# Wider output columns, interleaved memory heads and a reordered first projection in a fused two-stack transformer kernel

## The chip, the cores and the metric

The kernel runs on one core of a Trainium2 chip. The metric is the device time of one execution in microseconds; the value of a kernel is the median of several runs.

## What is computed

Two networks follow each other; the second takes the first one's output as its `x`. All weights and activations are fp32, 512 tokens of width 1024.

```python
# first block: one layer
h = rmsnorm(x, g_mix)
rq, rk, rv, rg, nq, nk, nv, xq, gate_logits = split(h @ w_in)
y_ret = (silu(rg) * groupnorm(retention(rq, rk, rv, forward and backward))) @ w_ret_o
y_na  = neighbourhood_attention(nq, nk, nv, na_rpb) @ w_na_o           # 8 heads of 64
y_xa  = cross_attention(xq, rmsnorm(mem, g_mem) @ w_mem_kv) @ w_xa_o   # 4 heads of 128, 256 memory rows
g_ret, g_na, g_xa = split(sigmoid(gate_logits))
x = x + (g_ret * y_ret + g_na * y_na + g_xa * y_xa) @ w_out
x = rmsnorm(x + moe(rmsnorm(x, g_ffn)), g_final)                       # 16 experts, 2 per token
# second block: two layers; ctx has 256 rows, x 512
for l in range(2):
    mod = silu(c) @ w_ada[l] + b_ada[l]          # shifts, scales, gates; the same for c_ctx
    h, hc = modulated rmsnorm of x and of ctx
    q, k, v of h and hc through w_in[l] (three attention kinds), joint attention over x and ctx
    x  = x + gate * rms(attention @ w_out[l])    # ctx too in layer 0
    x  = x + gate * rms(swiglu ffn)              # ctx too in layer 0
```

## The kernel before, in words

Every fp32 product is made of three: `split` (L87, lines 91 and 92) and `pair` (L73, lines 81 and 82) divide an operand into a high part, written by ACT, and a low part, written by DVE, and `mm3` (L97, lines 99 to 101) multiplies high by high, one high by low and low by high into one PSUM tile. A weight group is a 128x2048 block of 1 MB: SP's queue loads it into one of three `raw` buffers (L68), ACT makes `whi`, DVE makes `wlo` (three of each). `ahead` (L61) asks for a weight before its user is written. The loads of `ada` use the same `raw` buffers.

`tr` is a transpose on TensorE (PE, profile line 131). `mm` (L111) hands out PSUM tiles of 512 columns, one bank each. The code is written in an order, but a scheduler decides the order of each engine from the dependencies and the buffers; each engine then runs its own list in order. `skew` (L1412) writes the stages of a loop shifted against each other.

`bg` (L1329) runs one step of `ada` (L1260), a generator that computes the modulation vectors of the second block: a step loads 1 MB of `w_ada` and issues four products. `bg` is called at many places of the first block, so that these steps fill pauses.

The stages, with the time of the profiled execution:

- Retention to 235 us; its gate uses `proj_b` (L304), which makes 128 tokens by 256 columns with 24 products, then an eviction. Four groups of 256 columns, four token tiles each. `branch_out` (L491) to 320: for each group of 256 of the 1024 output columns, `proj_a` (L318) makes the gate, 128 columns by 512 tokens at a time, and the eviction adds the branch's own product (`bo`).
- Neighbourhood attention (`neighbourhood`, L538): `nv` by `proj_b` (370 to 395), then 16 `pairs` (L613: scores two steps ahead, softmax in `exps`, transposes `prt`, products with the values). Then `memory_rows` (L650) normalizes the memory rows on ACT and DVE, `rows_to_T` transposes the output, and `branch_out` for NA runs, with `memory_keys` (L666) in its middle (456 to 557). `memory_attention` (L693) projects `xq`, runs 8 `pairs` (582 to 612.5: `xs` scores, `prt`, `xpo`) and its own `branch_out`.
- `b1_out` (L731): `w_out` in four groups of 256 columns (687 to 738), with `context_T` between; routing; 16 experts (`experts`, L1111: gate and up products `eg`, transposes `et`, down products `ed`), 795 to 1101. Ahead of the last expert `gathered` runs, which asks for the gathered rows and calls `context_T` (L1453: transposes of 256 context rows and their modulation in `modulated`, L1355, lines 1369 to 1375). The combine adds expert rows (line 1077) and uses the context for first products of the second block.
- The second block: `project` (L1503), attention, `attn_out` (L1995), `ffn`, twice. In layer 1, six tiles of 128 rows (four of `x`, two of `ctx`) meet three groups of 256 columns first (7, 5 and 6), while the last turn of layer 0's `ffn` still delivers the normalized rows (`turn` at line 1352, transposes, `modulated`). That is 2156.7 to 2222. There `rows` is called for group 7 with tiles 0 to 3 and once more, with no weight given, for tiles 4 and 5, so its weight is loaded and split twice. Each of these weights is split in four steps of 512 columns:

```python
for g, ev in first:
    rows(g, range(4), ev)
    if g == 7:
        rows(g, range(4, 6), ev)
```

`attn_out` multiplies six (layer 0) or four (layer 1) tiles by `w_out2`, in four groups of 256 columns; `take` multiplies by a gate on DVE (line 2015) and `sumsq` squares on ACT (line 164).

Of the kernel before, what the change touches and what calls it, by code (L numbers as in the profile page):

```python
# [8 lines left out]
F = mybir.dt.float32  # L9
# [28 lines left out]
class Kern:  # L38
# [298 lines left out]
    def retention(self):  # L337
# [128 lines left out]
        for j in range(4):  # L466
            def evac(t, p, j=j):
                yy = y[:, t, j * 256:j * 256 + 256]
                th = self.t5("th", F, (256,))
                nc.scalar.activation(th, p, AF.Tanh, scale=0.5)  # L470
                sg = self.t5("sg", F, (256,))
# [19 lines left out]
    def branch_out(self, yT, nk, wname, gate_group, first=False, middle=lambda: None):  # L491
# [4 lines left out]
        for g in range(4):  # L496
            if g == 2:
                middle()
            if g * 256 % nw == 0:
                w = self.W(self.i[wname][g * 256 // nw, 0], k=nk)  # L500

            def evac(f, p, g=g, w=w):
                mx = self.mixT[:, 2 * g + f]
# [13 lines left out]
            self.proj_a(gate_group + g, evac)  # L517
# [20 lines left out]
    def neighbourhood(self):  # L538
# [13 lines left out]
        for c in range(2):  # L552
            self.proj_b(16 + c, lambda t, p, c=c: nc.scalar.activation(v[:, t, c * 256:c * 256 + 256], p, AF.Copy))
# [39 lines left out]
        self.pairs(16, scores, values, ("w_na_o", (0, 0), 4), ("w_in", (24, 0), 8), ("w_in", (25, 0), 8))  # L593
# [4 lines left out]
        oT = self.rows_to_T(o[:, ::-1])  # L598
        self.branch_out(oT, 4, "w_na_o", 24, middle=lambda: self.memory_keys(rows))
# [13 lines left out]
    def pairs(self, n, scores, values, *chunks):  # L613
# [5 lines left out]
        for i in range(n + 1):  # L619
# [17 lines left out]
            if i % 2 or n == 8:  # L637
                self.bg()
# [54 lines left out]
    def memory_attention(self):  # L693
# [29 lines left out]
        self.pairs(8, scores, values, ("w_xa_o", (0, 0), 4), ("w_in", (28, 0), 8), ("w_in", (29, 0), 8))  # L723
# [7 lines left out]
    def b1_out(self, *stages):  # L731
# [6 lines left out]
        self.xss = self.small.tile([128, 4, 4], F, name="xss", bufs=1)  # L738
# [4 lines left out]
        weight = lambda c: self.W(self.i["w_out"][c, 0], k=8)  # L743

        def product(t, c, w):
            p = self.mm("wo")[:, :256]
            for kt in range(8):
                ts = slice(t * 128, t * 128 + 128)
# [6 lines left out]
        for c in range(2):  # L755
            w = weight(c)
            for t in range(4):
                product(t, c, w)
# [1490 lines left out]
```

## Time and profile before

| what | us |
|---|---|
| median of three runs (lowest, highest) | 2984.36 (2974.34, 2985.76) |
| the profiled execution, its time and its span | 2978.37, 2976.6 |
| PE busy | 2847.3 |
| DVE busy | 1766.0 |
| ACT busy | 1293.1 |
| granted clock of PE, mean | 0.98 |

"Busy" of PE includes time in which a product is on its way; products overlap, so the step from one start to the next is the cost of one. The granted clock is the share of 2.4 GHz; 0.5 is 1.2 GHz. "[2.91 <-ACT hT L1374]" behind an instruction says that its engine stood idle for 2.91 us and that ACT's write of `hT` at line 1374 ended it. `x8` joins eight equal instructions.

### The profile page before, as it was taken

The page shows a single profiled execution, that of the slowest core. Times are in us where ns is not written, and L with a number is a line of the kernel's source. Part 1 is how long each engine was busy: PE and PEld are TensorE (multiplying, and loading weights), DVE is VectorE, ACT ScalarE, POOL GpSimd, SP SyncE. Part 2 cuts the span into 40 slices and gives each one's busy share as a digit, 9 for nine tenths or more (in the row PEclk, how much of TensorE's full clock was granted, in tenths as well). Part 3 has the DMA queues.
Part 4 walks back from the last instruction along what each step waited for, and adds up shares of the span by engine and source line. Part 5 has one row for each costly group of instructions (what it writes and reads, how often), then busy time and mean ns, then how long its engine had stood idle before and what let it go on. Part 6 is the DMA issues. An engine that isn't in the chain of part 4 may idle for free. (4 is left out here: it accounts for less than half of the span.)

```text
span 2976.6 us, 44654 instructions
## 1 busy us (share of the span) xinstructions
PE 2847.3 (96%) x17896; PEld 2463.2 (83%) x17896; DVE 1766.0 (59%) x3244; ACT 1293.1 (43%) x2272; POOL 214.7 (7%) x282
## 2 busy tenths in 40 slices
PE   8999999999799998899999999999989999899998
PEld 6997777779798978888889888888878878888887
DVE  6663244346588877688857343434566798644445
ACT  3222243234477765388845121112342787432222
POOL 2200000000110022111000000000010110000000
PEclk8999999999899999999999999999989999899999
DMA  5433454364799972431014111212233300322221
GB/s 202 142 131 132 153 198 185 144 234 151 260 390 385 380 269 96 155 84 28 4 57 156 57 71 57 71 57 71 79 126 117 109 23 2 128 106 107 86 98 71
DMA packets 130083, 399.77 MB, mean 134 GB/s; under 512 B 62199, under 2 KB 74887, under 8 KB 93128
## 3 DMA queue, kind: packets, MB, share of 16 engines
q1 hardware_dynamic: 116206, 350.04, 32.9%
q0 software_dynamic: 13520, 46.55, 4.7%
q8 instruction: 143, 2.34, 0.3%
q14 instruction: 70, 0.57, 0.1%
q10 hardware_dynamic: 144, 0.26, 0.0%
HBM read 356.64 MB, written 39.39 MB: 133 GB/s over the span
## 5 line engine op out<-in xcount | busy, mean ns | idle before, releaser
L82 DVE TENSOR_TENSOR wlo<-raw,whi 128x2048 fp32r<-128x2048 f32 (+1 forms) x200 | 420.5, 2104 | 292.1 <-ACT whi L81 291.7
L81 ACT ACTIVATE whi<-raw 128x2048 fp32r<-128x2048 f32 (+1 forms) x200 | 351.0, 1762 | 495.0 <-PE fd L101 132.2
L101 PE MATMUL fg<-hT,wlo 128*128 128x512 f32 (+1 forms) x1120 | 388.0, 347 | 0.0
L100 PE MATMUL fg<-hT,whi 128*128 128x512 f32 (+1 forms) x1120 | 387.8, 346 | 0.0
L99 PE MATMUL fg<-hT,whi 128*128 128x512 f32 (+1 forms) x1120 | 387.7, 347 | 0.0
L100 PEld LDWEIGHTS fg<-hT,whi 128*128 128x128 f32 x1120 | 212.3, 190 | 29.3
L99 PEld LDWEIGHTS fg<-hT,whi 128*128 128x128 f32 x1120 | 210.9, 189 | 29.4
L101 PEld LDWEIGHTS fg<-hT,wlo 128*128 128x128 f32 x1120 | 210.7, 188 | 29.0
L2099 DVE TENSOR_TENSOR sg<-sg,fg 128x512 f32<-128x512 f32 (+1 forms) x70 | 40.1, 573 | 284.6 <-PE fg L101 284.6
L92 DVE TENSOR_TENSOR pelo<-tp,pehi 128x512 fp32r<-128x512 f32 x260 | 175.0, 683 | 13.9 <-ACT pehi L91 11.8
L101 PE MATMUL fd<-whi,hl 128*128 128x512 f32 x440 | 174.0, 395 | 0.0
L100 PE MATMUL fd<-wlo,hh 128*128 128x512 f32 x440 | 173.5, 394 | 0.0
L99 PE MATMUL fd<-whi,hh 128*128 128x512 f32 x440 | 173.4, 394 | 0.0
L91 ACT ACTIVATE pehi<-tp 128x512 fp32r<-128x512 f32 x260 | 153.8, 601 | 44.9 <-PE tp L131 43.6
L2066 DVE TENSOR_TENSOR acc<-acc,fd 128x512 f32<-128x512 f32 x180 | 120.7, 685 | 68.2 <-PE fd L101 68.2
L1903 DVE TENSOR_REDUCE smx<-sn 128x1 f32<-128x768 f32 x160 | 151.7, 949 | 12.7 <-PE sn L1897 11.7
L131 PE MATMUL tp<-ident,pn 128*128 128x128 f32 x960 | 149.0, 274 | 1.6 <-DVE pelo L92 1.2
L1906 ACT ACTIVATE pn<-sn,smx 128x768 f32<-128x768 f32 x160 | 143.9, 904 | 9.2 <-DVE smx L1903 5.6
L99 PE MATMUL eg<-whi,xt 128*96 128x256 f32 x512 | 147.0, 287 | 0.0
L100 PE MATMUL eg<-wlo,xt 128*96 128x256 f32 x512 | 145.1, 283 | 1.0 <-DVE wlo L82 1.0
L101 PE MATMUL eg<-whi,xt 128*96 128x256 f32 x512 | 144.9, 283 | 0.0
L82 DVE TENSOR_TENSOR wlo<-rawx,whi 128x2048 fp32r<-128x2048 f32 x58 | 132.9, 2292 | 20.1 <-ACT whi L81 20.1
(655 smaller groups left out, 7305.6 us busy)
## 6 DMA issues: line engine op xcount, KB each, us to landing
raw<-in_w_in SPq DMA_DIRECT2D x53, 1024.0 KB, 4.9
raw<-in_w_ada SPq DMA_DIRECT2D x48, 1024.0 KB, 5.2
raw<-in_f_gate SPq DMA_DIRECT2D x22, 1024.0 KB, 4.8
raw<-in_f_up SPq DMA_DIRECT2D x22, 1024.0 KB, 4.8
raw<-in_f_down SPq DMA_DIRECT2D x22, 1024.0 KB, 4.8
rawx<-in_e_gate SPq DMA_DIRECT2D x19, 1024.0 KB, 9.0
rawx<-in_e_up SPq DMA_DIRECT2D x19, 1024.0 KB, 9.4
rawx<-in_e_down SPq DMA_DIRECT2D x18, 1024.0 KB, 8.9
```

Source lines behind the costliest of these rows:

```text
L81: keep(nc.scalar.activation(hi[:, c], raw[:, c], AF.Copy))
L82: keep((eng or nc.vector).tensor_tensor(lo[:, c], raw[:, c], hi[:, c].bitcast(F), op=OP.subtract))
L91: nc.scalar.activation(hi, src, AF.Copy)
L92: nc.vector.tensor_tensor(lo, src, hi.bitcast(F), op=OP.subtract)
L99: t.matmul(ps, lh, rh, start=first, stop=False)
L100: t.matmul(ps, lh, rl, start=False, stop=False)
L101: t.matmul(ps, ll, rh, start=False, stop=last)
L131: self.nc.tensor.transpose(out, in_, self.ident[:k, :k])
L1903: nc.vector.tensor_reduce(m[:, t:t + 1], p[:, :768], axis=AX.X, op=OP.max, negate=True)
L1906: nc.scalar.activation(P[t], p[:, :768], AF.Exp, bias=m[:, t:t + 1], accum_out=su[:, t:t + 1])
L2066: nc.vector.tensor_tensor(acc[:, t, cs], acc[:, t, cs], p, op=OP.add)
L2099: nc.vector.tensor_tensor(sg, sg, pp[1], op=OP.mult)
```

## The change

Line numbers grow by 8 early and by 54 to 62 later (L81 becomes L89, L91 becomes L99, L1128 becomes L1182, L1375 becomes L1430).

1. `W2` loads half of the k range of two weight groups into one `raw`, so that a product has 512 columns; the retention gate and `nv` (`proj_2`), `w_out` and `w_out2` in both layers use it.
2. `branch_out` becomes a generator, `branch_steps`. `memory_keys` stands directly behind the NA pairs, and NA's steps run between the `xa` pairs, two to a pair. `w_mem_kv` is asked for ahead in place of `w_na_o` and `w_in`. These steps call no `bg`.
3. `context_T` is called behind the last expert's transposes.
4. Layer 1's first projections put two tiles of 256 columns into one bank, load each of the three weights once, and do the context tiles of group 7 last.

```diff
+    def W2(self, aps, half):
+        raw = self.wp.tile([128, 2048], F, name="raw", tag="raw", bufs=self.NRAW)
+        c = slice(half * 1024, half * 1024 + 1024)
+        for a in range(2):
+            self.nc.sync.dma_start(raw[:, a * 1024:a * 1024 + 1024], aps[a][:, c])
+        return [x.rearrange("p (a k n) -> p k a n", a=2, k=4) for x in self.pair(raw)]
...
+    def proj_2(self, g, evac):
+        ps = []
+        for half in range(2):
+            w = self.W2([self.i["w_in"][g + a, 0] for a in range(2)], half)
+            for t in range(4):
+                if half == 0:
+                    ps.append(self.mm("prj"))
+                for k in range(4):
+                    kt = 4 * half + k
+                    self.mm3(ps[t].rearrange("p (a n) -> p a n", a=2), self.h(0, kt, t * 128, t * 128 + 128),
+                             self.h(1, kt, t * 128, t * 128 + 128), w[0][:, k], w[1][:, k], kt == 0, kt == 7)
+                if half == 1:
+                    evac(t, ps[t])
+            self.bg()
...
-            self.proj_b(8 + j, evac)
+            self.proj_2(8 + 2 * j, evac)
...
+    def branch_out(self, *args, **more):
+        for i, _ in enumerate(self.branch_steps(*args, **more)):
+            if i % 4 == 3:
+                self.bg()
+    def branch_steps(self, yT, nk, wname, gate_group, first=False):
...
+            wg = self.w_in(gate_group + g)
+            for f in range(2):
+                p = self.mm("prj")
...
+                yield
+                if f == 1 and g < 3:
+                    self.ahead(("w_in", (gate_group + g + 1, 0), 8))
+                mx = self.mixT[:, 2 * g + f]
                 py = self.mm("bo")
...
+                yield
...
-        self.pairs(16, scores, values, ("w_na_o", (0, 0), 4), ("w_in", (24, 0), 8), ("w_in", (25, 0), 8))
+        self.pairs(16, scores, values, beside, ("w_mem_kv", (0, 0), 8), ("w_mem_kv", (1, 0), 8), ("w_mem_kv", (2, 0), 8))
...
-        oT = self.rows_to_T(o[:, ::-1])
-        self.branch_out(oT, 4, "w_na_o", 24, middle=lambda: self.memory_keys(rows))
+        self.na_out = self.branch_steps(self.rows_to_T(o[:, ::-1]), 4, "w_na_o", 24)
+        self.memory_keys(rows)
...
-        self.pairs(8, scores, values, ("w_xa_o", (0, 0), 4), ("w_in", (28, 0), 8), ("w_in", (29, 0), 8))
+        def beside(i):
+            next(self.na_out, None)
+            self.bg()
+            next(self.na_out, None)
+        self.pairs(8, scores, values, beside)
+        for _ in self.na_out:
+            pass
+        self.ahead(("w_xa_o", (0, 0), 4), ("w_in", (28, 0), 8))
...
+        def turned_context():
             self.hc = self.context_T()
-        self.experts(idx, y_d, ahead, y15, spreading, gathered)
+        self.experts(idx, y_d, ahead, y15, spreading, gathered, turned_context)
...
         turn(prev[1], 1, prev[2])
+        behind_last()
...
+            def pairs(g, t0, ev, w):
+                p = self.mm("prj")
+                for a in range(2):
+                    ts = slice((t0 + a) * 128, (t0 + a) * 128 + 128)
+                    for kt in range(8):
+                        self.mm3(p[:, a * 256:a * 256 + 256], hT[0][:, kt, ts], hT[1][:, kt, ts], w[0][:, kt], w[1][:, kt],
+                                 kt == 0, kt == 7)
+                for a in range(2):
+                    ev(t0 + a, p[:, a * 256:a * 256 + 256])
+            ws = []
             for g, ev in first:
-                rows(g, range(4), ev)
-                if g == 7:
-                    rows(g, range(4, 6), ev)
+                ws.append(self.W(self.i["w_in2"][l, g], k=8, steps=4))
+                for t0 in (0, 2):
+                    pairs(g, t0, ev, ws[-1])
+            pairs(7, 4, ev_g, ws[0])
...
-        weight = lambda c: self.W(self.i["w_out2"][l, c], k=8)
+        weight = lambda c, half: self.W2([self.i["w_out2"][l, 2 * c + a] for a in range(2)], half)
```

`w_out` and the rest of `attn_out` change in the same way as `proj_2`: the four tiles (in layer 0 six) of the first 512 columns are open at once while the two halves of k pass, and the second 512 columns go tile by tile with both halves at hand; `take` adds or multiplies 512 columns at a time.

How the order of the instructions moves. First ACT in the `xa` pairs (`xpr` is the exponential, `prT` the copy of a transposed tile, `whi` a weight's high part, `gate` the tanh of a branch's gate). Before:

```order
L81 ACTIVATE whi<-raw 128x2048
L608 ACTIVATE xpr,ssu<-xs,snm 128x256 x2
L630 ACTIVATE prT<-prt 128x512
L1305 ACTIVATE adar<-ada 128x512
L608 ACTIVATE xpr,ssu<-xs,snm 128x256 x2
L630 ACTIVATE prT<-prt 128x512
L608 ACTIVATE xpr,ssu<-xs,snm 128x256 x2
L630 ACTIVATE prT<-prt 128x512
L81 ACTIVATE whi<-raw 128x2048
L608 ACTIVATE xpr,ssu<-xs,snm 128x256 x2
L630 ACTIVATE prT<-prt 128x512 x3
```

With the change:

```order
L645 ACTIVATE xpr,ssu<-xs,snm 128x256 x6
L667 ACTIVATE prT<-prt 128x512
L89 ACTIVATE whi<-raw 128x2048
L535 ACTIVATE gate<-prj 128x512
L645 ACTIVATE xpr,ssu<-xs,snm 128x256 x2
L667 ACTIVATE prT<-prt 128x512
L535 ACTIVATE gate<-prj 128x512
L645 ACTIVATE xpr,ssu<-xs,snm 128x256 x2
L667 ACTIVATE prT<-prt 128x512
L89 ACTIVATE whi<-raw 128x2048
L535 ACTIVATE gate<-prj 128x512
L645 ACTIVATE xpr,ssu<-xs,snm 128x256 x2
```

NA's gates and the splits of its weights now stand between the softmax steps, where there were two splits of weights for later stages and an eviction of `ada`.

DVE at the last expert (`eg` is the product of gate and up, `hidT` the low part of its transpose, `pre` and `hc` the context's modulation and its low part). Before:

```order
L1371 TENSOR_SCALAR pre<-trp,pre_a_3881,mod_566 128x128
L1128 TENSOR_TENSOR eg<-eg 96x256
L82 TENSOR_TENSOR wlo<-raw,whi 128x2048 x2
L1375 TENSOR_TENSOR hc<-pre,hc 128x4x128 x4
L1128 TENSOR_TENSOR eg<-eg 96x256
L92 TENSOR_TENSOR hidT<-et,hidT 128x192
L82 TENSOR_TENSOR wlo<-raw,whi 128x2048
L92 TENSOR_TENSOR hidT<-et,hidT 128x192
```

With the change:

```order
L90 TENSOR_TENSOR wlo<-raw,whi 128x2048 x3
L1182 TENSOR_TENSOR eg<-eg 96x256
L90 TENSOR_TENSOR wlo<-raw,whi 128x2048 x2
L1182 TENSOR_TENSOR eg<-eg 96x256
L100 TENSOR_TENSOR hidT<-et,hidT 128x192
L90 TENSOR_TENSOR wlo<-raw,whi 128x2048
L100 TENSOR_TENSOR hidT<-et,hidT 128x192
L1426 TENSOR_SCALAR pre<-trp,pre_a_3543,mod_566 128x128 x3
L90 TENSOR_TENSOR wlo<-raw,whi 128x2048
```

The four `hc` splits no longer stand ahead of the last `eg` product; the context's work follows the last `hidT`.

ACT in layer 1's first projections (`whi` in quarters is a weight of these projections, `pre` and `hT` belong to a row tile's turn, `sqj` to its norm). Before:

```order
L1374 ACTIVATE hT_15605<-pre 128x4x128 x2
L164 ACTIVATE sqj,pss_20822<-acc 128x1024
L1369 ACTIVATE pre<-trp,mod_3887,pre_a_5718 128x128 x4
L1374 ACTIVATE hT_15605<-pre 128x4x128 x2
L81 ACTIVATE whi<-raw 128x512 x4
L164 ACTIVATE sqj,pss_20878<-acc 128x1024
L81 ACTIVATE whi<-raw 128x512 x4
L1369 ACTIVATE pre<-trp,mod_3887,pre_a_5718 128x128 x4
L1374 ACTIVATE hT_15605<-pre 128x4x128 x2
```

With the change:

```order
L1429 ACTIVATE hT_15047<-pre 128x4x128 x2
L172 ACTIVATE sqj,pss_19932<-acc 128x1024
L1424 ACTIVATE pre<-trp,mod_3549,pre_a_11970 128x128 x4
L1429 ACTIVATE hT_15047<-pre 128x4x128 x2
L89 ACTIVATE whi<-raw 128x512 x4
L172 ACTIVATE sqj,pss_19988<-acc 128x1024
L1424 ACTIVATE pre<-trp,mod_3549,pre_a_11970 128x128 x3
L1588 ACTIVATE prj<-prj 128x128 x2
L1588 ACTIVATE prj<-prj 128x256
L1429 ACTIVATE hT_15047<-pre 128x4x128
```

One of the two sets of four splits ahead of the last tile's `pre` is gone.

## Rows read from the trace of the kernel before

**Rows 1.** Page, sections 1 and 2: busy time; granted clock by slice:
```profile
PE 2847.3 (96%) x17896; PEld 2463.2 (83%) x17896; DVE 1766.0 (59%) x3244; ACT 1293.1 (43%) x2272; POOL 214.7 (7%) x282
...
PEclk8999999999899999999999999999989999899999
```

**Rows 2.** Stretches: us, PE PEld DVE ACT POOL busy, clock, DMA share:
```profile
582.00:612.50 30.50, 27.93 (x200) 19.08 (x197) 16.65 (x37) 16.94 (x44) 2.57 (x5) 0.94 0.69 254
606.00:610.50 4.50, 3.72 (x19) 2.06 (x20) 0.82 (x3) 0.12 (x1) 0.00 (x0) 0.62 0.62 213
1101.00:1150.00 49.00, 41.15 (x276) 35.79 (x275) 40.29 (x110) 29.28 (x72) 1.85 (x3) 0.93 0.39 142
2156.70:2198.20 41.50, 27.43 (x168) 25.44 (x167) 34.21 (x104) 24.80 (x63) 5.49 (x11) 0.79 0.53 187
2198.20:2222.00 23.80, 23.80 (x204) 23.80 (x203) 7.85 (x11) 8.87 (x20) 0.00 (x0) 1.00 0.24 78
```

**Rows 3.** Timeline of PE (start, length, what): two products of `w_out`:
```profile
687.46 0.28 PE L99 MATMUL wo<-whi,mTh 128*128 128x256 f32 x1
...
693.33 0.28 PE L100 MATMUL wo<-wlo,mTh 128*128 128x256 f32 x1
```

**Rows 4.** Timeline of PE: two 512-column products of `proj_a`:
```profile
575.23 0.39 PE L101 MATMUL prj<-hTh,wlo 128*128 128x512 f32 x1
...
580.67 0.39 PE L101 MATMUL prj<-hTh,wlo 128*128 128x512 f32 x1
```

**Rows 5.** Tile `wo` and line 92 by form: min/median/max ns:
```profile
L2015 DVE TENSOR_TENSOR yB<-wo,gt x40: 412/424/425, 1539.5 to 2587.6; 128x256 f32<-128x256 f32 x40
...
L92 DVE TENSOR_TENSOR pelo<-tp,pehi x260: 644/681/694, 1268.1 to 2525.4; 128x512 fp32r<-128x512 f32 x130
```

**Rows 6.** Timeline of PE, `xa` pairs: [idle before <- what ended it]:
```profile
606.78 1.94 PE L1301 MATMUL ada<-raw,silu_c 128*32 128x512 f32 x8 [2.30 <-DMA raw<-in_w_ada]
```

**Rows 7.** Timelines of DVE and PE behind the NA pairs:
```profile
459.63 1.42 DVE L663 TENSOR_SCALAR xr<-xr,mem_y 128x1024 f32<-128x1024 f32 x2
...
454.58 1.92 PE L131 MATMUL trp<-ident,mix 128*128 128x128 f32 x16
```

**Rows 8.** Page, section 6: loads, issue to landing; lines 81, 82 by form:
```profile
raw<-in_w_in SPq DMA_DIRECT2D x53, 1024.0 KB, 4.9
raw<-in_w_ada SPq DMA_DIRECT2D x48, 1024.0 KB, 5.2
...
L81 ACT ACTIVATE whi<-raw x200: 612/1916/1966, 20.4 to 2939.2; 128x2048 fp32r<-128x2048 f32 x88, 128x512 fp32r<-128x512 f32 x12
...
L82 DVE TENSOR_TENSOR wlo<-raw,whi x200: 676/2292/2761, 30.6 to 2941.1; 128x2048 fp32r<-128x2048 f32 x88, 128x512 fp32r<-128x512 f32 x12
```

**Rows 9.** Timeline of PE where layer 0's attention starts:
```profile
1254.96 0.50 PE L1897 MATMUL sn<-mhi 96*128 96x512 f32 x1 [1.52 <-DVE mlo L92]
...
1258.61 0.83 PE L131 MATMUL tp<-ident,mqrow 128*96 128x128 f32 x6 [1.27 <-DMA mkrow<-p_d]
```

**Rows 10.** Timelines of DVE and PE at the last expert:
```profile
1089.72 2.52 DVE L1375 TENSOR_TENSOR hc<-pre,hc 128x512 fp32r<-128x512 f32 x4
1092.17 0.41 DVE L1128 TENSOR_TENSOR eg<-eg 96x256 f32<-96x256 f32 x1
...
1092.63 0.58 PE L131 MATMUL et<-ident,eg 96*128 96x96 f32 x2 [5.46 <-DVE eg L1128]
```

**Rows 11.** Layer 1's first projections: timeline of PE; DVE's costliest group:
```profile
2166.32 0.48 PE L99 MATMUL prj<-whi,hT 128*128 128x256 f32 x1 [2.91 <-ACT hT L1374]
...
2175.39 0.38 PE L99 MATMUL prj<-whi,hT 128*128 128x256 f32 x1 [3.28 <-ACT hT L1374]
...
2184.18 1.97 PE L131 MATMUL trp<-ident,raw 128*128 128x128 f32 x8 [3.18 <-DVE raw L1352]
...
2196.32 0.39 PE L99 MATMUL prj<-whi,hT 128*128 128x256 f32 x1 [1.12 <-ACT hT L1374]
...
L82 DVE TENSOR_TENSOR wlo<-raw,whi 128x512 fp32r<-128x512 f32 x12 | 8.2, 686 | 0.5 <-ACT whi L81 0.5
```

More of the change, by code (lines that the diff above doesn't have):

```diff
@@ L551, in neighbourhood @@
         v = self.s8("nv", [4, 512], F)
-        for c in range(2):
-            self.proj_b(16 + c, lambda t, p, c=c: nc.scalar.activation(v[:, t, c * 256:c * 256 + 256], p, AF.Copy))
+        self.proj_2(16, lambda t, p: nc.scalar.activation(v[:, t], p, AF.Copy))
         vs = self.s8("nvs", [3, 512], F)
@@ L611, in exps, with pairs @@
         return rec
-    def pairs(self, n, scores, values, *chunks):
+    def pairs(self, n, scores, values, beside, *chunks):
         nc = self.nc
@@ L636, in pairs @@
                 chunks = chunks[1:]
-            if i % 2 or n == 8:
-                self.bg()
+            beside(i)
     def rows_to_T(self, o):
@@ L721, in values, with beside @@
                                     rec[:, :, None].to_broadcast([128, 2, 128]), op=OP.mult)
[L723 removed]
+        def beside(i):
+            next(self.na_out, None)
+            self.bg()
+            next(self.na_out, None)
[3 more added lines that the diff above has]
+        self.ahead(("w_xa_o", (0, 0), 4), ("w_in", (28, 0), 8))
         if self.stop == "xa":
@@ L742, in b1_out, with weight, product, take @@
         self.context_rows()
[L743 to L748, printed above, removed]
-                self.mm3(p, mT[0][kt // 4][:, kt % 4, ts], mT[1][kt // 4][:, kt % 4, ts], w[0][:, kt], w[1][:, kt],
+        def weight(c, half):
+            return self.W2([self.i["w_out"][2 * c + a, 0] for a in range(2)], half)
+        def product(p, t, half, w):
+            ts = slice(t * 128, t * 128 + 128)
+            for k in range(4):
+                kt = 4 * half + k
+                self.mm3(p.rearrange("p (a n) -> p a n", a=2), mT[0][half][:, k, ts], mT[1][half][:, k, ts], w[0][:, k], w[1][:, k],
                          kt == 0, kt == 7)
-            cs = slice(c * 256, c * 256 + 256)
+        def take(p, t, c):
+            cs = slice(c * 512, c * 512 + 512)
             nc.vector.tensor_tensor(xr[t][:, cs], p, xr[t][:, cs], op=OP.add)
-            self.sumsq(xr[t][:, cs], 256, self.xss[:, t, c:c + 1])
-        for c in range(2):
-            w = weight(c)
+            self.sumsq(xr[t][:, cs], 512, self.xss[:, t, c:c + 1])
+        ps = [self.mm("wo") for _ in range(4)]
+        for half in range(2):
+            w = weight(0, half)
             for t in range(4):
-                product(t, c, w)
+                product(ps[t], t, half, w)
+                if half == 1:
+                    take(ps[t], t, 0)
         self.hc = self.context_T()
-        ws = [weight(c) for c in (2, 3)]
+        ws = [weight(1, half) for half in range(2)]
         def products(t):
-            for c in (2, 3):
-                product(t, c, ws[c - 2])
+            p = self.mm("wo")
+            for half in range(2):
+                product(p, t, half, ws[half])
+            take(p, t, 1)
         self.ahead(("w_in2", (0, 0), 8))
@@ L1109, in next_weight, with experts @@
         return w
-    def experts(self, idx, y_d, ahead, y15, middle, before_last):
+    def experts(self, idx, y_d, ahead, y15, middle, before_last, behind_last):
         nc, n = self.nc, self.CAP
@@ L2037, in products @@
         def products(t):
-            for c in (2, 3):
-                p = self.mm("wo")[:, :256]
-                for kt in range(8):
-                    mms(p, ws[c - 2], t, kt)
-                take(p, t, c)
+            p = self.mm("wo")
+            for kt in range(8):
+                mms(p, ws[kt // 4], t, kt)
+            take(p, t, 1)
         self.skew(nq, products, lambda t: turns.append(self.post(l, "a", t, o[:, t], ss[:, t], xs[t], hT)),
```

49 lines of the change are left out of this document (21 added, 28 removed).

## The prediction

> **What bounds the kernel now.** I read the page first: TensorE (PE) is busy 96% of the span, DVE 59%, ACT 43% [rows 1]. So time can come from three sources only: from PE's own instructions, from the few places where PE stands still, or from stretches at a low clock; a slice that shows 7 or 8 in place of 9 has lost clock [rows 1]. Next I read the timeline of PE stage by stage, and then the table of stretches for those that the change touches [rows 2]. There the picture is not that of the mean. In layer 1's first projections (2156.7 to 2198.2) PE is busy 27.4 of 41.5 us at a mean clock of 0.79, and DVE 34.2: DVE sets that stretch. In the `xa` pairs (582.0 to 612.5) no engine is full and PE ends them late. In the combine (1101 to 1150) DVE is busy 40.3 of 49 us, nearly as long as PE. In the first projections behind the last turn (2198.2 to 2222.0) PE never stops [rows 2].
>
> The profiled execution took 2978.37 us; the three timed runs have a median of 2984.36. The four together have a mean of 2980.7, and from that the sum is taken. 0.5% is 14.9 us, about what a measurement of this kernel can tell from no change; beyond that I call it faster or slower.
>
> **Part A, 512 columns.** It removes 1920 products of 256 columns (384 in the retention gate, 192 in `nv`, 384 in `w_out`, 576 and 384 in layers 0 and 1 of `attn_out`) and adds 960 of 512. The products overlap, so their cost is the step from start to start, not the printed length. 49 steps lie between the two rows of `w_out`: 5.87 us, 0.1198 each [rows 3]. 24 steps lie between the two rows of `proj_a`: 5.44 us, 0.2267 each [rows 4]. Two narrow ones less one wide one give 0.0129 us; the first block has 480 such pairs: 6.2 us. In layer 1 the narrow step is shorter, 23.8 us for 204 [rows 2], 0.1167, which leaves 0.0067 a pair and 3.2 us for the 480 pairs of `attn_out`. Against it, what follows a last product is longer: a take of 256 columns lasts 0.42 us on DVE, an operation on 512 columns 0.68 [rows 5]. Only the ends of `w_out` and the two `attn_out` have nothing behind them, 0.3 to 0.5 us each with ACT's half of it: 1.3. The weights arrive as two half loads in place of one, with equal bytes and an equal number of splits, so nothing else changes. A = -6.2 - 3.2 + 1.3 = **-8** (-9 to -5).
>
> These rows are at odds with a rule. The Trainium skill ("TensorE: Matmul & The Clock Gate", section "Back-to-back issue gap") puts the step at the columns over 2.4 GHz plus about 2.5 ns; by it a pair would give only 2.5 ns, all 960 together 2.4 us. The trace disagrees: its narrow step is some 10 ns above that page's. The sum goes by the rows; the other outcome is a rival.
>
> **Part B, memory heads and NA's output.** In the order of the change, gates of the NA branch stand between the softmax steps of the `xa` pairs. What those pairs can give back: 30.5 us now hold 2.57 idle [rows 2], of which 2.30 at one place, waiting for a `w_ada` load [rows 6], and a stretch of 4.5 us at 0.62 that loses 1.7 [rows 2]: at least 4.3. At most: 48 products of `xs`, 32 transposes and 64 `xpo` at 0.12 are 17.3, and 56 `ada` products at half the 1.94 us for 8 of [rows 6] (they ran at 1.2 GHz) are 6.8: 24.1 of 30.5, so 6.4. I take -6, since 24 to 28 us of NA's own products now fill the pauses.
>
> New is an exposed chain. Behind the NA pairs the memory keys come at once, and their transposes need rows that line 663 scales until 461.05, two times 0.74 behind the NA evictions of DVE, while the transposes of `o` end at 456.50 [rows 7]. Today NA's gate products cover this. Two `ada` groups of about 0.97 each remain as cover, so PE stands some 2.6 us; a pause of 2.3 was followed by 1.7 us of lost clock above. Between +1 (the scaling goes earlier without the NA splits in front) and +5: +3.5.
>
> The NA steps do not call `bg`, so four calls are missing and two `ada` steps come late, in the first products of layer 0's attention. On SP's queue the `w_ada` load of the second stands between the `p_d` stores; its buffer is that of the first. A load lands 5.2 us after its issue [rows 8]; PE waits for 2 to 3 of these, and runs 1 us of products and 1.3 of copy and transposes. It absorbs the 1.52 and 1.27 that PE waits there now [rows 9]. Behind PE stand `sn` and everything after. 2.5 + 2.3 - 2.8 = +2 (0 to +4). B = -6 + 3.5 + 2 = **-0.5** (-6 to +5).
>
> **Part C, context behind the last expert.** Now DVE's four `hc` splits (1089.72 to 1092.17) stand ahead of the product that PE's `et` transposes wait for: PE is idle 5.46 us [rows 10]. In the new order that product follows directly on a `wlo` split, so `et` comes up to 2.5 us earlier, and 16 context transposes cover 1.9 of the next wait. But the same DVE work, 8 x 0.4 of `pre` and 4 x 0.65 of `hc`, goes into the combine, where DVE has 8.7 us left of 49 [rows 2], behind two additions of rows (1.3 each) and a split of 2.29 [rows 8]. If all of it lands on the path it costs 5.8, if none, the gain is 4. Take **0** (-4 to +5).
>
> **Part D, layer 1's first projections.** The three groups are 336 products: 39.2 us at 0.1167; with 32 transposes at 0.12 [rows 7] that is 43.0 of 65.3 us [rows 2]. 22.3 us are lost: PE waits for `hT` or for the scaled rows again and again, 2.91, 3.28, 3.18 and 1.12 us [rows 11], and the clock falls. DVE paces it. The change removes the second load of group 7, with it four splits on DVE, 2.7 us of the 8.2 there [rows 11], and four of 0.61 on ACT [rows 8]. In the order they stand right before the last turn's scaling, so its transposes come that much earlier. And it puts more products ahead of that turn: 193 stand before the last transposes where 110 stood, filling pauses that were there anyway; 143 are left behind them. DVE's 34.2 less 2.7, plus the 2 to 5 us that it must still wait for ACT and PE, puts the last `hT` at 2190 to 2193; 143 x 0.1167 = 16.7 more gives 2207 to 2210 in place of 2222. If DVE's wait is covered entirely, PE alone needs 43 us: 2200. So -12 to -15, -22 at the best; at the worst the 2.7 of the splits and the last pause, -4. Take **-15**, since products that fill pauses also keep the clock up. Two tiles in one bank make the eviction of the first wait for the second's 24 products, 2.8 us, but nothing on PE waits for these evictions; the stops above are all for `hT`.
>
> A rule speaks against it: the Trainium skill ("Perfetto Trace Analysis", section "Matmuls") wants independent groups in different banks, so that the eviction of one runs beside the next group. If PE had to wait 2.8 us for each of the seven pairs, 19.6 us would eat the gain; no row here shows PE waiting for a bank in this stretch.
>
> **Sum.** -8 - 0.5 + 0 - 15 = -23.5; 2980.7 - 23.5 = 2957.
>
> **The rivals.**
> 1. DVE paces the first projections as before, and a wait takes the place of the one removed: D gives its worst value, -4, A its -8, B and C together +2. -10: **2971**, no change by the bound. For it: DVE's 31.5 us of work remains in front of the last `hT`. Against: the pauses that PE has there are filled by its own products.
> 2. Slower. Between the `xa` pairs, NA's six weights (four `w_in`, two `w_na_o`) are loaded just ahead of use: 4.9 to land, 1.92 to split on ACT and 2.29 on DVE [rows 8] are 9.1 us, and a step has less than 6 us of PE work ahead of it. If SP issues each only when its user is next, 6 x 9.1 = 54.6 us are exposed in place of the 6 gained: 2980.7 - 8 + 5.5 - 15 + 54.6 gives **3018**. It decides where the issue stands under 9.1 us ahead of the first product. Against it: three raw buffers let the issue run ahead of the splits, and DMA's share in the pairs is 0.69 with room left [rows 2].
> 3. The wide step gives only 2.4 us in all, as by the rule in part A: -17.9, **2963**. Against it are the two rows' steps; the chance stands for a narrow step that the trace shows too long in stages where PE waits for something else.
> 4. D and B come out at their best, -22 and -6: -8 - 6 - 22 = -36, **2945**.
>
> **How the numbers follow.** Forecast 0.56, rival 1 0.20, rival 2 0.05, rival 3 0.12, rival 4 0.07. Rivals 3 and 4 and the forecast lie beyond 14.9 us: faster 0.75; rival 1 is the same: 0.20; slower 0.05. The forecast's own range comes from the bounds of B, C and D, about 12 to either side: 2945 to 2969. The range given takes in rivals 1, 3 and 4 and the spread of the runs (2974 to 2986) about the base: 2938 to 2975; rival 2 and some edges of the others are outside.
>
> **What would show it.** A: the wide step at 0.227, and `w_out` shorter by 2.5 us. B: PE without a stop in the `xa` pairs, a pause of 2 to 3 us behind NA's transposes, and two `ada` groups after 1240 us. C: the stop before the last `et` at about 3 us, and the combine no longer than its 49 us. D: two sets of four narrow splits in place of three, and the first projections in 47 to 53 us in place of 65. The prediction is wrong if the first projections still take over 60 us, or if PE shows stops of over 5 us before NA's products between the pairs.

## The result, and the profile after

The changed kernel takes 2966.18 us (median of 19 runs, 2957.86 to 2975.78); before, measured beside it, 2980.93 (19 runs). The ratio is 0.9949, 95% interval 0.9937 to 0.9961: 14.8 us less (11.6 to 18.8), against 23.5 forecast and inside the stated range. A second measurement of the same program, in the last series below, gave 0.9979 (0.9964 to 0.9994), 6 us less. The two intervals do not meet, so two series of the same program can differ by more than an interval says. The change is a gain, and it is smaller than the forecast.

The profiled execution has a span of 2964.5 us, 12.1 less than before. The page, sections 1 and 2:

```profile
PE 2839.2 (96%) x16936; PEld 2412.8 (81%) x16936; DVE 1760.1 (59%) x3196; ACT 1284.1 (43%) x2200; POOL 219.3 (7%) x282
...
PEclk8999999999899999999999999999999999899999
```

The 960 instructions fewer on PE are those of part A, and the slices with a low clock are one fewer [rows 1]. That says little of where the time went. I put stages side by side by the starts and ends of their products in the two timelines of PE:

| stage, by PE's products | before | after | change | forecast |
|---|---|---|---|---|
| A: retention gate, first product to the transposes of its output | 56.0 | 53.6 | -2.4 | -2.5 |
| A: `nv`, with the NA projections | 76.2 | 75.0 | -1.2 | -1.25 |
| B: last `npo` to last `xpo` (memory, `xq`, `xa` pairs; NA's output also lies here) | 158.0 | 152.3 | -5.6 | -2.5 |
| A: `w_out`, first to last product | 49.7 | 53.4 | +3.8 | -2.5 and a tail |
| C: first `gt` to last `ed` (experts) | 306.1 | 299.5 | -6.7 | 0 for C in all |
| C and B: last `ed` to the first score of layer 0 | 153.9 | 168.7 | +14.9 | +2 for B |
| A: `attn_out`, layer 0, to the first `fg` | 79.5 | 77.3 | -2.2 | -1.9 and a tail |
| D: the 336 first products of layer 1 | 65.3 | 46.4 | -18.9 | -15 |
| A: `attn_out`, layer 1, to the first `fg` | 61.6 | 63.5 | +1.9 | -1.3 and a tail |

Six lines went about as forecast or better, and three did not: `w_out`, the start of layer 0's attention, and the end of layer 1's `attn_out`. The stretches of the changed kernel that answer to [rows 2]; columns as there:

```profile
510.50:605.10 94.60, 93.80 (x516) 71.74 (x516) 35.44 (x63) 26.83 (x55) 2.57 (x5) 1.00 0.44 165
680.50:734.00 53.50, 49.21 (x223) 41.03 (x220) 33.07 (x76) 19.93 (x37) 4.75 (x9) 0.94 0.46 177
2158.60:2205.00 46.40, 43.81 (x372) 42.35 (x371) 39.21 (x109) 30.18 (x75) 5.88 (x11) 1.00 0.49 173
```

In the `xa` pairs with NA's products between them PE now stands for 0.8 of 94.6 us, at full clock. The first projections (2158.6 to 2205.0) have PE busy 43.8 of 46.4 us at full clock, where it was 27.4 of 41.5 at 0.79 in the first part alone. `w_out` (680.5 to 734.0) lost 4.3 us to standing and some of its clock; before, the stop at the same place was 0.31 us:

```profile
711.27 1.97 PE L131 MATMUL trp<-ident,x 128*128 128x128 f32 x16 [0.31 <-DVE x L1451]
```

The timeline of PE in the changed kernel, at the places where terms of the sum stand:

```profile
459.43 1.72 PE L139 MATMUL trp<-ident,xr 128*128 128x128 f32 x14 [1.49 <-DVE xr L699]
...
702.16 0.39 PE L109 MATMUL wo<-whi,mTl 128*128 128x512 f32 x1
706.83 3.68 PE L139 MATMUL trp<-ident,x 128*128 128x128 f32 x16 [4.29 <-DVE x L1506]
...
1083.33 0.38 PE L139 MATMUL et<-ident,eg 96*128 96x96 f32 x2 [1.13 <-DVE eg L1182]
...
1256.54 1.06 PE L1356 MATMUL ada<-raw,silu_c 128*32 128x512 f32 x8 [2.52 <-DMA raw<-in_w_ada]
1258.38 1.11 PE L139 MATMUL ada<-ident,adar 128*128 128x128 f32 x4 [0.77 <-ACT adar L1360]
1259.77 0.80 PE L1965 MATMUL sn<-mhi 96*128 96x512 f32 x1 [0.28 <-DVE mod L1365]
...
2166.49 0.39 PE L107 MATMUL prj<-whi,hT 128*128 128x256 f32 x1 [1.33 <-ACT hT L1429]
...
2183.30 1.09 PE L139 MATMUL trp<-ident,raw 128*128 128x128 f32 x8 [0.96 <-DVE b_y L159]
...
2577.44 1.94 PE L139 MATMUL trp<-ident,raw 128*128 128x128 f32 x8 [6.05 <-DVE post_t L163]
```

The stop for the memory rows is 1.49 us (2.6 were reckoned). The stop ahead of the last `et` went from 5.46 [rows 10] to 1.13. The four long stops of layer 1's first projections [rows 11] are one of 1.33 and one of 0.96. New are 4.29 us ahead of the context transposes in `w_out`, and 2.52 and 0.77 around an `ada` step ahead of the first score. The stop behind layer 1's `attn_out`, 4.55 us before, is 6.05.

The wide step of `w_out` is what [rows 4] said; 24 steps between these two rows of PE are 5.45 us, 0.2271 each:

```profile
681.75 0.40 PE L109 MATMUL wo<-whi,mTl 128*128 128x512 f32 x1
...
687.20 0.39 PE L109 MATMUL wo<-whi,mTl 128*128 128x512 f32 x1
```

In the `attn_out` of layer 1 it is longer, 14 steps in 3.26 us, 0.2329 each:

```profile
2567.73 0.40 PE L107 MATMUL wo<-whi,hT 128*128 128x512 f32 x1
...
2570.99 0.40 PE L109 MATMUL wo<-whi,hT 128*128 128x512 f32 x1
```

### The profile page after: what moved, and what is told of

Its sections match the earlier page's. It is cut to its first block, busy times and chain, and to the rows that moved or that the text cites. A ratio compares the mean times of both kernels' runs of the same rounds, so it can differ in the third digit from the quotient of the medians.

```text
span 2964.5 us, 42595 instructions
## 1 busy us (share of the span) xinstructions
PE 2839.2 (96%) x16936; PEld 2412.8 (81%) x16936; DVE 1760.1 (59%) x3196; ACT 1284.1 (43%) x2200; POOL 219.3 (7%) x282
## 5 line engine op out<-in xcount | busy, mean ns | idle before, releaser
L89 ACT ACTIVATE whi<-raw 128x2048 fp32r<-128x2048 f32 (+1 forms) x196 | 349.2, 1785 | 504.1 <-PE fd L109 132.3
L99 ACT ACTIVATE pehi<-tp 128x512 fp32r<-128x512 f32 x260 | 153.8, 601 | 48.4 <-PE tp L139 47.0
L1971 DVE TENSOR_REDUCE smx<-sn 128x1 f32<-128x768 f32 x160 | 151.8, 949 | 14.4 <-PE sn L1965 13.5
## 6 DMA issues: line engine op xcount, KB each, us to landing
rawx<-in_e_up SPq DMA_DIRECT2D x19, 1024.0 KB, 10.4
```

Of the source, the lines that this page charges most:

```text
L89: keep(nc.scalar.activation(hi[:, c], raw[:, c], AF.Copy))
L99: nc.scalar.activation(hi, src, AF.Copy)
L1971: nc.vector.tensor_reduce(m[:, t:t + 1], p[:, :768], axis=AX.X, op=OP.max, negate=True)
```

## The experiments

The first four take one part of the change each and put it alone on the kernel before. The edits are the parts of the diff ahead of the prediction.

**Part A alone.**

```diff
+ W2, proj_2, w_out and attn_out in 512 columns; all else as before
```

> Part A alone (512 columns in the retention gate, nv, w_out and both attn_out). The forecast's working: 8 us less than before, w_out itself 2.5 us shorter. The rival read from the profile of the changed kernel: w_out does not get shorter but 3 to 4 us longer, because its first half is over before the context rows are normalized and PE stops 4 us ahead of the context transposes; then the whole is 0 to 4 us less than before.

Measured: 2966.67 us, ratio 0.9966 (0.9952 to 0.998), 10 us less (6 to 14). `w_out` took 47.85 us, 1.8 less than before, with a stop of 1.25 us at the same place; timeline of PE:

```profile
706.99 1.97 PE L139 MATMUL trp<-ident,x 128*128 128x128 f32 x16 [1.25 <-DVE x L1482]
```

So A gives what was forecast when it stands alone, and the stop in `w_out` is there already, but short. The rival's number (0 to 4) is excluded for A alone. In the profile its own stages come to some 7 us less: gate 2.5, `nv` 1.2, `w_out` 1.8, `attn_out` 3.2 less in layer 0 and 1.5 more in layer 1.

**Part B alone.**

```diff
+ branch_steps; memory_keys behind the NA pairs; NA's steps between the xa pairs
```

> Part B alone (memory heads first, NA's branch between the xa pairs). The forecast's working: within 1 us of before, the pairs giving 6 and the memory rows and two late ada steps taking 5.5. The rival: the pairs and the memory heads together give about 5 to 6 us, but the two late ada steps take 6 to 8 at the start of layer 0's attention; the whole is 0 to 4 us more than before.

Measured: 2978.15 us, ratio 1.0004 (0.9988 to 1.0021), no change; the forecast's -0.5 and the rival's 0 to 4 both lie inside. The profile tells the parts apart. From the last `npo` to the last `xpo` it takes 154.5 us, 3.4 less than before. At the start of attention the second late step shows as in the changed kernel:

```profile
1254.14 1.31 PE L1322 MATMUL ada<-raw,silu_c 128*32 128x512 f32 x8 [2.16 <-DMA raw<-in_w_ada]
1256.20 1.11 PE L131 MATMUL ada<-ident,adar 128*128 128x128 f32 x4 [0.75 <-ACT adar L1326]
1257.60 0.80 PE L1918 MATMUL sn<-mhi 96*128 96x512 f32 x1 [0.28 <-DVE mod L1331]
```

The products and transposes of the two late steps together; window, then busy time of PE on the tile `ada` alone, clock and DMA:

```profile
1240.00:1262.00 22.00, 4.53 (x20) 0.77 0.65 192
```

From the last combine product to the first score it takes 133.5 us, before 127.3: +6.2; at the end of layer 0's attention 4.6 of it are left. The forecast had +2, so here the rival's mechanism holds, at a lower net price than it named.

**Part C alone.**

```diff
+ context_T called by behind_last(), no longer by gathered()
```

> Part C alone (context transposed behind the last expert). The forecast's working: no change, 4 less to 5 more. The rival read from the changed kernel: the last expert ends 6 to 7 us earlier, the combine gives 3 back, and 3 to 4 us stay as a gain.

Measured: 2977.42 us, ratio 0.9993 (0.9977 to 1.0009): no change that can be told. In the profile the experts take 298.5 us in place of 306.1 (-7.6), and from the last `ed` to the first score it is 161.5 in place of 153.9 (+7.6). The stop ahead of the last `et` is 0.67 us, where it was 5.46 [rows 10]:

```profile
1084.43 0.39 PE L131 MATMUL et<-ident,eg 96*128 96x96 f32 x2 [0.67 <-DVE eg L1130]
```

What PE wins there it gives back behind the last `ed`, about half by standing and half by a lower clock. From there to the first score, before and in part C alone:

```profile
1101.07:1254.96 153.89, 139.08 (x1046) 132.08 (x1044) 114.19 (x313) 66.49 (x158) 21.95 (x24) 0.97 0.38 130
...
1092.34:1253.87 161.53, 143.03 (x1046) 135.46 (x1045) 119.46 (x322) 68.95 (x163) 24.61 (x26) 0.94 0.39 140
```

PE stands 3.7 us more, and is busy 3.9 us more with as many instructions. The stretch that begins with the last `ed` and ends with the last combine product, first of the kernel before:

```profile
1101.00:1128.00 27.00, 25.40 (x169) 20.65 (x167) 20.74 (x43) 14.85 (x34) 0.76 (x1) 1.00 0.52 191
```

and then of part C alone, where DVE has become the engine that is as busy as PE:

```profile
1092.40:1121.80 29.40, 26.27 (x168) 20.97 (x168) 26.27 (x55) 16.73 (x39) 3.39 (x3) 1.00 0.67 264
```

DVE's busy time grew by 5.5 us there, about the 5.8 of context work that the prediction moved. The forecast of 0 holds, and the work came onto the path as it said; but each of the two sizes is larger than the prediction's most (a gain of 4, a cost of 5.8), and they cancelled.

**Part D alone.**

```diff
+ pairs(g, t0, ev, w); each weight once; pairs(7, 4, ev_g, ws[0]) last
```

> Part D alone (layer 1's first projections in pairs of tiles, each weight loaded once, context tiles of group 7 last). The forecast's working: 15 us less, these projections in about 50 us. The rival: PE itself sets the stretch, 20 us less, projections in 45 us, no stop over 2 us in it.

Measured: 2959.94 us, ratio 0.9938 (0.9915 to 0.996), 18.5 us less (12 to 25). The first projections took 50.4 us, 14.9 less, with one long stop of 3.57 and one of 1.29. The timeline of PE at the longer, and then the busy times of the stretch:

```profile
2157.42 0.41 PE L99 MATMUL prj<-whi,hT 128*128 128x256 f32 x1 [3.57 <-ACT hT L1374]
```

```profile
2147.20:2197.60 50.40, 45.54 (x370) 44.77 (x369) 39.38 (x109) 30.04 (x74) 5.52 (x11) 0.97 0.46 161
```

In its place (50 us) the forecast is right. The changed kernel's 46.4 is 4 us less with the same order, of which 2.2 are that first stop (3.57 against 1.33); the clock (0.97 against 1.00) and the narrow step (0.117 against 0.1135 in the two profiles, 1.2 us over 336) cover the rest. By their medians the four parts alone add up to some 30 us less (10, -1, 2 and 18.5), and together they gave 15 or 6. The next runs look for what stands between them.

**The missing background steps run between the `xa` pairs.**

```diff
             next(self.na_out, None)
-            self.bg()
+            self.bg(1 + i % 2)
             next(self.na_out, None)
```

> The changed kernel with one more background step in every second of the eight xa pairs, so that no ada step is left for layer 0's attention. If the two late ada steps are what the start of attention loses: no ada products behind 1000 us, the first score product of layer 0 comes 6 to 8 us earlier than in the changed kernel against the end of the last combine product, and the xa pairs grow by the 4 us of the four steps at most. If they only took the place of waits that were there anyway (the forecast's +2): 2 us earlier or less.

One execution, 2958.96 us. No `ada` product is left behind 1000 us. From the last combine product to the first score it takes 132.7 us, in the changed kernel 138.9: 6.2 less, as the first theory said. But from the last `npo` to the last `xpo` it takes 159.5 us, 7.2 more than in the changed kernel, where at most 4 were expected. The whole span is 7.4 us less all the same: layer 0's `ffn`, where not one instruction differs (last section), takes 6.1 less, and `w_out`, whose code is the same too, 5.7 less. It takes 47.7 us here, and the stop ahead of the context transposes is short:

```profile
706.64 1.97 PE L139 MATMUL trp<-ident,x 128*128 128x128 f32 x16 [1.10 <-DVE x L1506]
```

So the late steps are the cause of the wait at the start of attention, and moving them here does not pay for them: PE is full in those pairs. And the 4.29 us in `w_out` are not a fixed price of the changed kernel.

**The context rows first.**

```diff
+        self.context_rows()
         for t in range(4):
             nc.gpsimd.dma_start(xr[t], self.i["x"][t])
-        self.context_rows()
```

> The changed kernel with the two context rows loaded and normalized ahead of the four rows of x in the stage of w_out. If w_out lost its gain to the late context rows: the stop of 4.3 us ahead of the context transposes is gone, and the stage from the first to the last product of w_out takes 47 to 48 us in place of 53.4. If it is something else (splits of the weights late on ACT and DVE), the stop stays over 3 us.

One execution, 2948.32 us. `w_out` takes 46.5 us with PE busy in all of it, and the context transposes follow the products without a stop. Timeline of PE, and busy times of the stage:

```profile
700.88 1.91 PE L139 MATMUL trp<-ident,x 128*128 128x128 f32 x16
```

```profile
679.00:725.50 46.50, 46.50 (x222) 38.80 (x219) 30.17 (x73) 19.57 (x36) 4.20 (x8) 1.00 0.55 204
```

That is 3.1 less than before and 6.9 less than in the first profile of the changed kernel: the theory's numbers. Against the 47.7 us of the run above it is 1.2 less. The timeline of ACT shows where the rows were late; in the changed kernel the squares of both context rows wait for their loads:

```profile
699.50 1.06 ACT L172 ACTIVATE sqj<-x 128x1024 bf16<-128x1024 f32 x1 [5.83 <-DMA x<-in_ctx]
701.99 1.06 ACT L172 ACTIVATE sqj<-x 128x1024 bf16<-128x1024 f32 x1 [1.33 <-DMA x<-in_ctx]
```

in the kernel before, whose `w_out` starts 7 us later, they stand here:

```profile
705.45 1.06 ACT L164 ACTIVATE sqj<-x 128x1024 bf16<-128x1024 f32 x1 [4.01 <-DMA x<-in_ctx]
...
706.70 1.06 ACT L164 ACTIVATE sqj<-x 128x1024 bf16<-128x1024 f32 x1
```

and with the context first they are done 6 us earlier, measured from the first product of `w_out`:

```profile
693.16 1.06 ACT L172 ACTIVATE sqj<-x 128x1024 bf16<-128x1024 f32 x1 [9.12 <-DMA x<-in_ctx]
694.23 1.06 ACT L172 ACTIVATE sqj<-x 128x1024 bf16<-128x1024 f32 x1
```

**Only the second load of group 7 removed.**

```diff
-                rows(g, range(4), ev)
+                w = rows(g, range(4), ev)
                 if g == 7:
-                    rows(g, range(4, 6), ev)
+                    rows(g, range(4, 6), ev, w)
```

> The kernel before with only the second load and split of group 7 removed; order and banks as before. The forecast's working has DVE as the pace and 2.7 us of splits in front of the last turn: the first projections 3 to 4 us shorter. The rival: the gain of part D is from the order (products that stand ahead of the last turn), so 0 to 2 us here.

One execution, 2974.42 us. The first projections take 64.0 us, 1.3 less than before: inside the rival's 0 to 2. It is no gain that can be told, since with these projections unchanged they took 63.0, 63.8 and 63.9 us in parts A, B and C alone. The stops stay, the longest of them in front of the last turn:

```profile
2163.65 0.39 PE L99 MATMUL prj<-whi,hT 128*128 128x256 f32 x1 [3.24 <-ACT hT L1374]
...
2172.71 0.38 PE L99 MATMUL prj<-whi,hT 128*128 128x256 f32 x1 [3.04 <-ACT hT L1374]
...
2182.10 1.97 PE L131 MATMUL trp<-ident,raw 128*128 128x128 f32 x8 [3.78 <-DVE raw L1352]
```

DVE's 2.7 us less do not show: the last turn's transposes end 35.2 us behind the first product, where it was 37.3 before, but 35.8 to 35.9 in parts A, B and C alone. And PE had fewer products ahead of their end (103, else 112).

**The new order, one tile to a bank.**

```diff
-                rows(g, range(4), ev)
-                if g == 7:
-                    rows(g, range(4, 6), ev)
+                w = rows(g, range(4), ev)
+                w7 = w if g == 7 else w7
+            rows(7, range(4, 6), ev_g, w7)
```

> The kernel before with each weight loaded once and the context tiles of group 7 last, but one tile to a bank as before. If two tiles to a bank cost or give nothing, the first projections take what they take in the changed kernel (46 us from the first product to the end of the 336); if a shared bank delays evictions that matter, they are shorter here; if the pairs' wider turns are what keeps PE busy, this one stays at 55 us or more.

One execution, 2971.02 us. The first projections take 54.9 us, 10.4 less than before (8 to 9 less than in parts A, B and C alone) and 4.5 more than with pairs. 133 products stand ahead of the end of the last turn's transposes, with pairs 195, before 112. So the order brings 8 to 10 us and the pairs 4.5; the removed load by itself brings nothing that can be told. With pairs more products stand ahead of the last turn. That two tiles to a bank let the scheduler hold more of them open is how I read it; the free banks were not counted, so this is not shown.

**The changed kernel again, and three versions beside it.** All four stood beside the same 28 runs of before.

> The changed kernel once more, beside the next ones on one chip. Against before about 15 us less, as measured. Its profile tells whether the step of equal products in layer 0's ffn belongs to the program (then it is that of the first profile: 118.5 ns for 256 columns, 233 for 512) or to the single execution (then it can be another, such as 116 and 229).

> The changed kernel with the context rows ahead of x, timed. If the late context rows took w_out's gain, it is 6 to 8 us faster than the changed kernel beside it: 21 to 23 us less than before. If the 18 us between the two profiles came mostly from another step of the products, the two are within 4 us of each other.

> The same, with the four missing background steps run at the start of the routing, where PE is idle for some 15 us. If the late ada steps cost 4 to 6 us net: 4 to 6 us faster than with the context rows alone, the first score product of layer 0 about 128 us behind the last combine product in place of 138. If the loads of w_ada push the first experts' weights back, the first expert starts later by as much and nothing is gained.

> The changed kernel with the context rows ahead of x and with the context transposed ahead of the last expert as before (part C undone). If part C gives nothing (forecast), it is within 4 us of the kernel with part C; if C gives what its profile shows alone, 3 to 4 us, it is slower by that.

The third and the fourth stand on the second:

```diff
         self.b1_out(norm, turned, logits)
+        self.bg(4)
```

```diff
                     self.gather(g2[t][:, k], y_d, main[k][0][:, t, :1])
+            self.hc = self.context_T()
...
         turn(prev[1], 1, prev[2])
-        behind_last()
```

| kernel | median us | ratio to before (95%) |
|---|---|---|
| changed, again | 2970.17 | 0.9979 (0.9964 to 0.9994) |
| context rows first | 2959.79 | 0.9937 (0.9915 to 0.9958) |
| and `bg(4)` in the routing | 2956.71 | 0.9941 (0.9922 to 0.9961) |
| context first, part C undone | 2961.17 | 0.9948 (0.9931 to 0.9965) |

In this series context rows first beats the changed kernel beyond both intervals, and takes 16 to 19 us off before (18.8 by the ratio), where 21 to 23 were expected. In the profiles `w_out` takes 49.7 us in the changed kernel this time, with a stop of 2.9 us, and 46.7 with the context first; that is 3 of the 10 us between the medians, and in the first pair of profiles it was 6.9. The rest is not settled, and that the two lines cause it is not shown: by the ratio the changed kernel differs by some 9 us from its own first measurement (0.9949), and its profiled execution here (2953.36 us) is the fastest of its 14, faster than the profiled one with the context first (2955.60).

With `bg(4)` in the routing the late steps are gone (the first score 132.5 us behind the last combine product, 138.1 without), but the first expert starts later behind `w_out` (61.6 us, 58.7 without), for the gathered rows:

```profile
786.98 1.51 PE L139 MATMUL gt<-ident,xy 96*128 96x96 f32 x8 [12.19 <-DMA xy<-h_d,ridx]
```

By the ratio it is the same as without; 4 to 6 us less had been expected. Part C undone changes nothing either: 0.9948 against 0.9937.

**The parts and the whole, by stages.** I added up, in each profile, the stages in which a part has its instructions (the table above, with the stretch on to layer 0's `attn_out` for B). Against before, A alone comes to -7.3 us, B to +1.5, C to 0 and D to -14.9: 20.7 less. The changed kernel comes to 18.0 less over the same stages in its first profile and to 24.4 less in its second. So the gap between 30 and 15 or 6 does not show in the stages. In the first profile the rest of the kernel takes 5.9 us more, nearly all of it in stages that no part touches, and so 18.0 less becomes 12.1. What lengthens the other executions of the second series, whose median lies 17 us above the profiled one, no trace shows.

## Why the prediction was right, and where its sum failed

**Direction and range were right**, and so were the largest term and its mechanism. The time alone could not show it: 2966 lies nearer to rival 3 (2963) and to rival 1 (2971) than to 2957, its 14.8 us stand just at the 14.9 beyond which the prediction speaks of faster, and the 6 us of the second measurement lie well below that; taken from 2980.7 they come out at the upper edge of the range. That the time fell on this side is in part luck. The stages tell the rivals apart. Rival 1 needed D at -4, rival 4 D at -22 together with B at -6; rival 2 fails on 0.8 us of standing in 94.6 between the `xa` pairs. Point by point:

- *D, -15.* Measured -14.9 alone (-12.6 to -13.5 against parts A, B and C alone) and -18.9 in company. That products ahead of the last turn fill its pauses is what `d_order` shows (-8 to -10). What the prediction put on the removed splits was mis-sized: it had the last turn 2.7 us earlier and counted that as gain; alone it gave nothing that can be told. The low clock of the stretch went with the stops (0.79 to 1.00), as said. The rule of the Trainium skill ("Perfetto Trace Analysis", section "Matmuls") that wants independent groups in different banks, so that an eviction runs beside the next group, was not the limit here: with two tiles to a bank the stretch was 4.5 us shorter than with one.
- *A, -8.* Alone -10 (-14 to -6). In the first block the step of 0.227 held to a thousandth of a microsecond. In `attn_out` the wide step was 0.233 and the narrow one 0.118, not 0.2267 and 0.1167; the products of the two still took 2.2 and 0.7 us less, near the 3.2 reckoned. Rival 3 is out: its 2.4 us for all 960 wide products is what the gate's 192 gave. The formula behind that rival, columns over 2.4 GHz plus about 2.5 ns, is given by the Trainium skill ("TensorE: Matmul & The Clock Gate", section "Back-to-back issue gap") for an isolated product; of a stream in which each product has its own weight load the section says that at few columns the formula comes out too low. On that the traces agree with the page, where the prediction has them disagree: 0.120 in `w_out` and 0.1135 to 0.118 in layer 1, where the formula's estimate is 0.109. At 512 columns the section has such a stream at some 131 ns; the 227 and 233 ns measured here disagree.
- *A in company is the step that failed.* The sentence "with equal bytes and an equal number of splits, so nothing else changes" took no account of the work that `w_out`'s products were covering. The chain load, square, root, scale, transpose of the context rows had ended just under the narrow products (0.31 us of stop); the wide ones are over sooner. In the first profile the second row's load came late as well: its square starts 21.5 us behind the first product, before 19.2, though the load was issued 1.1 us sooner. PE stood 4.29 us, in the second profile 2.9, with the background steps moved 1.1, and in the first it lost clock behind that. Against -2.5, `w_out` cost +3.8, 0 and -2.0 in the three; why the load lands late in one execution and not in another is open. The prediction named what follows the products in `w_out`, and not what ran beside them.
- *B, late `ada` steps, +2.* +6.2 at the first score, +4.6 at the end of the attention. The old waits of 1.52 and 1.27 [rows 9] did go, as the working had it: 0.28 stands ahead of the first `sn`, and nothing ahead of the transposes of `mqrow`. What it left out is PE's own time for the first of the two steps. It counted 1 us of products and 1.3 of copy and transposes; the `ada` products and transposes of both steps keep PE busy for 4.53 us, and the copy stands beside that. B's other terms were near: the pairs and the memory rows gave -3.4 to -5.6 together where -2.5 was reckoned, and the whole of B is nothing, 1.0004.
- *C, 0.* Right, by way of -7.6 and +7.6. The mechanism is the one given, the sizes are not: 4 was the most that it was to gain and 5.8 the most that it was to cost, the stop ahead of the last `et` was to be about 3 us and is 0.67 alone and 1.13 in the changed kernel, and the clock on either side was not in the sum. That the two came out equal is luck.
- *The tails.* Layer 1's `attn_out` was to gain 1.3 less a tail of some 0.5; it lost 1.9. The stop behind it grew from 4.55 to 6.05 us. A tail was reckoned for the wider take and its square, and they do add some 0.5 us. The most of it, 1.2 us, is that DVE starts the take later behind the last product, because it is still at the `hT` splits of another tile. The last product on PE and what DVE does then, before and after:

```profile
2586.70 0.28 PE L101 MATMUL wo<-whi,hT 128*128 128x256 f32 x1
...
2586.44 1.29 DVE L1375 TENSOR_TENSOR hT<-pre,hT 128x512 fp32r<-128x512 f32 x2
2587.64 0.42 DVE L2015 TENSOR_TENSOR yB<-wo,gt 128x256 f32<-128x256 f32 x1
...
2570.99 0.40 PE L109 MATMUL wo<-whi,hT 128*128 128x512 f32 x1
...
2572.05 1.29 DVE L1430 TENSOR_TENSOR hT<-pre,hT 128x512 fp32r<-128x512 f32 x2
2573.26 0.68 DVE L2083 TENSOR_TENSOR yB<-wo,gt 128x512 f32<-128x512 f32 x1
```

Together the three that failed are some 0.5 to 6, 2.6 and 2.7 us on the wrong side, and D is 4 on the right one. That makes 2 to 8 of the 9 us between 2957 and 2966; the rest is within what two measurements of the same program differ by.

## What to carry to other kernels

When products get faster, look at what they covered: the loads and the chains that ended just under them are the next stop, and moving such a load to the front of its queue can be worth more than the wider products of that stage (here two lines, 1 to 7 us of `w_out` in the profiles). Where one engine paced another turn by turn, putting the other's work ahead of the last turn gave 8 to 10 us, and taking work off the pacing engine nothing that can be told. And a change in several parts has to be looked at stage by stage, alone and in company: by the medians these four gave 30 us one by one and 6 to 15 together, by their stages 21 and 18 to 24.

## What was not expected of the hardware

The step of equal products differs from execution to execution. In the window from 1700 to 1900 us PE is busy throughout, at full clock, in layer 0's `ffn`, on instructions that no experiment changed. The kernel before:

```profile
1700.00:1900.00 200.00, 200.00 (x1049) 170.23 (x1048) 75.87 (x92) 38.36 (x44) 0.00 (x0) 1.00 0.18 64
```

the changed kernel:

```profile
1700.00:1900.00 200.00, 200.00 (x1049) 170.00 (x1048) 75.16 (x91) 38.08 (x44) 0.00 (x0) 1.00 0.18 64
```

and the same program in its second profile:

```profile
1700.00:1900.00 200.00, 200.00 (x1060) 171.04 (x1059) 75.82 (x92) 38.51 (x44) 0.00 (x0) 1.00 0.18 64
```

1049 products in 200 us are 0.1907 each, 1060 are 0.1887: over the whole `ffn` the one program takes 561.3 and then 555.3 us. Of the other profiles four have about the first value and seven the second, and it does not go with the part that was changed: the changed kernel shows both, and part D alone, which changes nothing ahead of layer 1, has the other step than the kernel before. So 6 us of any difference between two profiles can be this, and they have to be compared stage by stage. What sets it is open.
